# Block products for layer B's input projection from the third head pair on, with their operand sums made in the second pair

## The chip, the cores and the metric

The kernel runs on one core of one Trainium2 chip. The metric is device time in microseconds (us) of one execution, median of several runs. The engines are named as in the profile: PE is the matrix engine (PEld is its loading of the stationary operand), DVE the vector engine, ACT the scalar engine, POOL GpSimd, SP the engine whose queue issues every DMA of this kernel.

## The reference

Two attention layers, each `x + W_out(attn(RMSNorm(x)) * silu(gate))`, on a prompt of 2048 tokens and a sample of 64 tokens, model width 1024:

```python
def project(x, norm_g, w_in, q_g, k_g, n_heads, n_kv):
    h = rms_norm(x, norm_g)
    p = h @ w_in
    q, k, v, gate = jnp.split(p, [wq, wq + wkv, wq + 2 * wkv], axis=-1)
    q = rms_norm(q.reshape(*lead, n_heads, HEAD_DIM), q_g)
    k = rms_norm(k.reshape(*lead, n_kv, HEAD_DIM), k_g)
    ...
def gated_attention_layer(...):
    qp, kp, vp, gp = project(x_p, norm_g, w_in, q_g, k_g, n_heads, n_kv)
    op = prompt_band_attention(qp, kp, vp, past_chunks, bias_fn, sinks)
    y_p = x_p + (op * jax.nn.silu(gp)) @ w_out
    # the same for the sample, against its caches
```

Layer A has 16 query heads on 2 key heads and a window of three chunks of 64 tokens; layer B has 16 heads with keys and values of their own and a window of nine chunks. The new keys and values are outputs too. The change is in layer B's `h @ w_in`, the product of 2112 tokens by 1024 by 4096.

## The kernel before, in words

**Numbers in two parts.** Every large product is made in 32-bit floats split into a high part (rounded to the engine's fast format, `F32R`) and a low part (the rest). `x @ w` is then three products, high by high, high by low and low by high, summed in PSUM. ACT makes the high part, POOL (activations) or DVE (weights) the low part.

**Work of layer B.** The tokens lie in *units*: eight of 256 tokens (two tiles of 128) and one of 64 (the sample, `NU`). `order` is units 0 to 6, the sample, unit 7. The heads go in eight *pairs* (`hp` 0 to 7). One *item* is a unit of a pair, 72 in all. For an item the projection (`project_b`, L513 to L536) makes 512 columns for each tile: 128 of q, k, v and gate each. A tile takes 8 steps of 128 input features with three matmuls each (L527, L528, L529), 48 matmuls of 512 columns for a unit. The activations are the stationary operand, the weights the moving one. The finished tile is evacuated from PSUM by two ACT reads (`evacuate`, L635), then normed and gated.

**Operands.** `load_b` (L542 to L596) loads them. In the first pair each unit's four blocks (two tiles by two halves of the features, named A11, A12, A21, A22) are loaded from layer A's result `x1` into `xraw` (L579), split (L553, L554) into an `xx` buffer and stored split in the DRAM tensor `xo` (L555). Later pairs load the four blocks from `xo` (L549), 512 KB each. There are seven `xx` buffers (`XN`), five of `xraw` (`XR`), three of `wraw` (`WB`), fifteen each of `wh` and `wl` (`WN`).

**Weights.** `load_weights` (L282 to L341) brings a pair's weights in eight chunks of 128 x 512; ACT scales each by the norm's gain and rounds it (L315), DVE makes the low part (L318). Eight of the fifteen buffers hold a pair, so seven chunks of the next pair can be made before the present pair has let go of anything. The first five are given out three jobs early (`EARLY`, `WP`), the rest in the job before.

**Order.** PE's order is written out by the program: attention of an item is taken in steps (`scores` L1244, `values` L1304, `outputs` L1324, driven by `pipeline`), and between two steps a `Filler` emits projection steps up to a mark, so that an item's projection ends two items before its attention. `PACE_B` is the filler work per head and tile. The other engines and the SP queue are ordered by a scheduler. Small jobs for ACT, DVE and POOL wait in a background queue (`bg`) and are given out between the steps of attention. SP's queue is taken in order: what stands behind a DMA that waits, waits too.

**Attention of an item.** For each tile and head: scores into a PSUM buffer of the two named `sb` (L1274, L1275), DVE adds the bias and finds the extremum (L1281), ACT exponentiates (L1285), PE transposes (L743), and a copy brings the result from PSUM (L1321: ACT for the first tile of the unit, DVE for the second). Then the values are multiplied (L1347) and the result goes by way of DVE (L1353) to DRAM.

Of the kernel before, what the change touches and what calls it, by code (L numbers as in the profile page):

```python
# [9 lines left out]
F32 = mybir.dt.float32  # L10
# [5 lines left out]
P = 128  # L16
# [19 lines left out]
XN = 7  # L36
EARLY = 3
# [16 lines left out]
def hybrid_encoder_kernel(  # L54
# [174 lines left out]
    xo = dr.tile([P, 4 * NU + 1, 8 * P], F32, tag="xo", name="xo")  # L229
# [306 lines left out]
    SLOT = {n: i for i, n in enumerate(("A11", "A12", "A21", "A22"))}  # L536
# [5 lines left out]
    def load_b(unit, hp):  # L542
# [13 lines left out]

        if T == TS:
            if hp:
                x.joint = cached("J", 4 * NU)[:, : 8 * P].rearrange("p (k s) -> p k s", k=8)
                return x  # L560
# [3 lines left out]
            def fn():  # L564
                xx = t("xx", [P, 4 * OT], XN, F32R)
                x.joint = v = xx[:, : 8 * P].rearrange("p (k s) -> p k s", k=8)
                split(xx, v[:, :, :TS], v[:, :, TS:], raw, 4 * NU)
# [4 lines left out]
        names = ("A11", "A12", "A21", "A22")  # L572
        raw = {}

        def raws():
            for e in range(2):
                for i in range(2):
                    r = t("xraw", [P, 2 * OT], XR)[:, :512].rearrange("p (k s) -> p k s", k=4)
                    held["last"] = load(r, x1[:, 4 * i : 4 * i + 4, u * UT + e * P : u * UT + e * P + P]).ins  # L579
                    raw["A%d%d" % (e + 1, i + 1)] = r  # L580

        def part(n, src):
            def fn():
                xx = t("xx", [P, 4 * OT], XN, F32R)
                xh, xl = operand(xx)
                split(xx, xh, xl, raw[src], 4 * u + SLOT[n])
                x.op[n] = xh, xl
            return fn

        if hp == 0:  # L590
            raws()
            x.items = [bg.put(0.52, part(n, n)) for n in names]
        else:
            for n in names:
                x.op[n] = operand(cached(n, 4 * u + SLOT[n]))
# [538 lines left out]
    def layer_b():  # L1134
# [4 lines left out]
        def add_unit(hp, unit):  # L1139
# [13 lines left out]
            def weights(*m):  # L1153
                if hp not in st.emit:
                    (st.w[hp],), _, st.emit[hp] = load_weights(1, (w_in_b[hp], 512))
# [41 lines left out]
            filler.total += 8 * (6 if T == UT else 2) * 512 / 2400  # L1197
            it.mark = filler.total
            filler.add(prefetch, weights if u == 0 else None, gen)
# [104 lines left out]
        def values(it, i, h):  # L1304
# [15 lines left out]
            copy = (nc.scalar.copy, nc.vector.tensor_copy)[i]  # L1320
# [36 lines left out]
        def pipeline():  # L1357
# [10 lines left out]
            for x, it in enumerate(its):  # L1368
# [3 lines left out]
                if x + 2 < len(its):  # L1372
                    near = its[x + 2].mark
# [215 lines left out]
```

## Time and profile before

| | |
|---|---|
| median of 3 runs | 2264.24 us (2262.56 to 2265.06) |
| the profiled execution's own time | 2262.1 us |
| its span in the profile | 2260.3 us |
| granted PE clock, mean | 0.997 |
| PE, DVE, ACT, POOL busy | 99%, 63%, 58%, 34% of the span |
| layer B's projection (L527 to L529) | from about 858 us on |
| output projection at the end | about 2110 to 2260 us |

The profile is one execution; times in its views count from the start of the span. Matmuls are pipelined and their ends are modelled, so what a matmul costs is read from the distance between the starts of two that follow each other, not from its duration.

### The profile page before, as it was taken

The numbers are of one execution on the slowest core, as the hardware profiler recorded it, in microseconds if no ns is written. First come the engines' busy times: TensorE is split into PE (matmuls) and PEld (weight loads), VectorE is DVE, ScalarE is ACT, GpSimd is POOL, SyncE is SP. The second block draws the span as 40 slices with busy tenths as digits, with TensorE's granted clock in tenths as the row PEclk, the third lists the DMA queues.
The fourth block names the chain that finished last, engine by engine and source line by source line (L and its number), as shares of the span: only waits on it lengthen the run. The fifth ranks groups of instructions, "written<-read, shape, count | busy, mean of one in ns | idle before, by whom it ended". The sixth has DMA issues, their size and how long they took to land. (4 is left out here: it accounts for less than half of the span.)

```text
span 2260.3 us, 41004 instructions
## 1 busy us (share of the span) xinstructions
PE 2231.6 (99%) x13981; PEld 1908.7 (84%) x13981; DVE 1423.0 (63%) x4168; ACT 1312.7 (58%) x3341; POOL 778.4 (34%) x1153
## 2 busy tenths in 40 slices
PE   8999999999999999999999999999999999999999
PEld 7887888888889998878888888888888888888999
DVE  7779988888785545675655655656556556565211
ACT  7888877777774335664555655545556555454321
POOL 5654533333254445431222222222222212223442
PEclk9999999999999999999999999999999999999999
DMA  8846446754446767554554544544545445443664
GB/s 281 298 144 214 165 139 184 224 179 146 158 121 193 215 188 268 186 182 142 150 148 138 158 139 142 151 145 142 148 140 160 138 137 154 139 125 113 201 182 135
DMA packets 236800, 379.26 MB, mean 168 GB/s; under 512 B 24288, under 2 KB 167024, under 8 KB 236560
## 3 DMA queue, kind: packets, MB, share of 16 engines
q1 hardware_dynamic: 236592, 376.65, 54.4%
q8 instruction: 110, 1.80, 0.3%
q14 instruction: 98, 0.80, 0.1%
HBM read 296.13 MB, written 82.08 MB: 167 GB/s over the span
## 5 line engine op out<-in xcount | busy, mean ns | idle before, releaser
L527 PE MATMUL pj<-wh,xx 128*128 128x512 f32 x1024 | 426.8, 417 | 0.0
L529 PE MATMUL pj<-wh,xx 128*128 128x512 f32 x1024 | 403.6, 394 | 0.0
L528 PE MATMUL pj<-wl,xx 128*128 128x512 f32 x1024 | 403.3, 394 | 0.0
L1285 ACT ACTIVATE p<-p,nm 128x640 f32<-128x640 f32 (+5 forms) x272 | 204.4, 751 | 236.9 <-DVE nm L1281 234.1
L1281 DVE CUSTOM_DVE_ANT_0 p<-sb,BT 128x640 f32<-128x640 f32 (+5 forms) x272 | 196.5, 722 | 173.3 <-PE sb L1275 169.5
L1441 PE MATMUL pj<-xx,wh 128*128 128x264 f32 x1024 | 295.0, 288 | 4.9 <-DVE res L1446 4.8
L389 POOL TENSOR_TENSOR xx<-xraw,xx 128x528 fp32r<-128x528 f32 (+1 forms) x168 | 225.1, 1362 | 202.9 <-ACT xx L388 197.4
L1442 PE MATMUL pj<-xx,wh 128*128 128x264 f32 x1024 | 292.1, 285 | 0.0
L1443 PE MATMUL pj<-xx,wl 128*128 128x264 f32 x1024 | 290.8, 284 | 0.0
L654 POOL TENSOR_TENSOR f<-f,mhalf 128x4 f32<-128x4 f32 (+1 forms) x136 | 137.4, 1011 | 428.9 <-DVE f L653 420.6
L613 PE MATMUL pj<-wh,xx 128*128 128x512 f32 (+1 forms) x624 | 245.9, 394 | 1.3 <-ACT pb L635 1.0
L614 PE MATMUL pj<-wl,xx 128*128 128x512 f32 (+1 forms) x624 | 233.0, 373 | 1.8 <-DVE wl L318 1.8
L615 PE MATMUL pj<-wh,xx 128*128 128x512 f32 (+1 forms) x624 | 234.1, 375 | 0.0
L527 PEld LDWEIGHTS pj<-wh,xx 128*128 128x128 f32 x1024 | 193.0, 188 | 44.9 <-issue 20.1
L529 PEld LDWEIGHTS pj<-wh,xx 128*128 128x128 f32 x1024 | 192.7, 188 | 44.8
L528 PEld LDWEIGHTS pj<-wl,xx 128*128 128x128 f32 x1024 | 193.7, 189 | 23.2
L1441 PEld LDWEIGHTS pj<-xx,wh 128*128 128x128 f32 x1024 | 193.6, 189 | 7.8 <-DVE res L1446 6.0
L635 ACT ACTIVATE pa<-pj,rms 128x384 f32<-128x384 f32 (+1 forms) x219 | 118.1, 539 | 136.7 <-PE pj L529 125.8
L1442 PEld LDWEIGHTS pj<-xx,wh 128*128 128x128 f32 x1024 | 193.3, 189 | 0.2
L1443 PEld LDWEIGHTS pj<-xx,wl 128*128 128x128 f32 x1024 | 193.5, 189 | 0.0
L388 ACT CAST xx<-xraw 128x528 fp32r<-128x528 f32 (+1 forms) x168 | 103.0, 628 | 133.0 <-PE pj L1443 112.9
L1040 ACT ACTIVATE p<-p,nm 128x257 f32<-128x257 f32 (+2 forms) x272 | 134.5, 497 | 73.5 <-DVE nm L1034 61.3
(228 smaller groups left out, 5222.1 us busy)
## 6 DMA issues: line engine op xcount, KB each, us to landing
xx<-xo SPq DMA_DIRECT2D x231, 512.0 KB, 3.6
xx<-xsa SPq DMA_DIRECT2D x88, 512.0 KB, 4.6
xraw<-oga SPq DMA_DIRECT2D x64, 264.0 KB, 3.5
xo<-xx SPq DMA_DIRECT2D x33, 512.0 KB, 4.4
xraw<-ogb SPq DMA_DIRECT2D x64, 264.0 KB, 3.4
xsa<-xx SPq DMA_DIRECT2D x32, 512.0 KB, 4.2
wraw<-in_w_in_b_dram SPq DMA_DIRECT2D x64, 256.0 KB, 3.1
xraw<-in_x_dram SPq DMA_DIRECT2D x40, 256.0 KB, 4.6
```

What stands on the lines that cost most here:

```text
L389: nc.gpsimd.tensor_tensor(xl, rv, xh.bitcast(F32), op=ALU.subtract)
L527: nc.tensor.matmul(ps, xh, wh, start=k == 0, stop=False)
L528: nc.tensor.matmul(ps, xh, wl, start=False, stop=False)
L529: nc.tensor.matmul(ps, xl, wh, start=False, stop=k == KC - 1)
L613: nc.tensor.matmul(ps[:n, :C], xh, wh, start=k == 0, stop=False)
L614: nc.tensor.matmul(ps[:n, :C], xh, wl, start=False, stop=False)
L615: nc.tensor.matmul(ps[:n, :C], xl, wh, start=False, stop=k == KC - 1)
L1281: mi = nc.vector.tensor_tensor_reduce(out=p[:n, :nk], in0=S[:n, o : o + nk], in1=bias[:n, b0 : b0 + nk], op0=ALU.add, op1=ALU.min, scale=1 ...
L1285: ex = nc.scalar.activation(p[:n, :nk], p[:n, :nk], AF.Exp, scale=-1.0, bias=nmh, accum_out=it.sm[:n, 2 * i + h : 2 * i + h + 1],)
L1441: nc.tensor.matmul(ps[:, :OT], wh, oh, start=k == 0, stop=False)
L1442: nc.tensor.matmul(ps[:, :OT], wh, ol, start=False, stop=False)
L1443: nc.tensor.matmul(ps[:, :OT], wl, oh, start=False, stop=k == KC - 1)
```

## The change

The first two pairs (`PLAIN = 2`) are projected as before. From the third pair on, a unit of 256 tokens by 1024 features by 512 columns is treated as a 2 x 2 by 2 x 2 block product and made of seven block products instead of eight (the Strassen-Winograd form). A block product is 4 steps of 3 matmuls with 256 columns, 84 matmuls of 256 columns for a unit. The operands are four sums of the activation blocks (S1 to S4) beside A11, A12 and A22, and four sums of the weight blocks (T1 to T4) beside 11, 21 and 22.

- **Activation sums.** In the second pair each unit's four raw blocks are loaded again from `x1`, DVE makes the four sums in place (L676 of the new file), they are split and stored to slots 4 to 7 of `xo`. A unit's loads are put into the background queue when the next unit is prefetched, and its sums one unit later (`mixed`). From the third pair on a unit loads seven operands of 512 KB instead of four, through the same seven `xx` buffers.
- **Weights.** `block_weights` loads eight raw blocks (three in `wraw`, five in `xraw`), ACT scales block 12 (L588), DVE mixes them in place (L579, 16 half blocks), and seven pieces of two halves are split (ACT L565 or L570, DVE L566 or L571). A pair holds 14 of the 15 buffers.
- **Evacuation.** Two PSUM buffers `pj` take turns, and products of the two tiles share partial sums: P1 is read twice by ACT (once with each tile's scale), P6 and P7 once, P2 once as the result for tile 0's q and k; POOL adds P1 to P6 and to P7; DVE reads P5, P4 and P3 with an addition. P2 goes on top of P1 in its buffer, P7 on top of P6, P4 on top of that, P3 on top of P5.
- **The sample** is made block by block with the same weights, 32 matmuls of 256 columns instead of 16 of 512.
- From the third pair on ACT makes all four copies of L1321, and the pace is 0.875 of `PACE_B`.

```diff
+    def product(ps, xc, parts, p, start):
+        xh, xl = xc.op[OPERAND[p]]
+        for k in range(4):
+            wh, wl = parts(PIECE[p], k)
+            nc.tensor.matmul(ps[:, :256], xh[:, k], wh, start=start and k == 0, ...)
+            nc.tensor.matmul(ps[:, :256], xh[:, k], wl, start=False, ...)
+            nc.tensor.matmul(ps[:, :256], xl[:, k], wh, start=False, ...)
...
+        def sums(u):
+            for dst, a, b, op in (
+                ("A22", "A21", "A22", ALU.add), ("A21", "A11", "A21", ALU.subtract),
+                ("A11", "A22", "A11", ALU.subtract), ("A12", "A12", "A11", ALU.subtract),
+            ):
...
+                    nc.vector.tensor_tensor(raw[dst], raw[a], raw[b], op=op)
...
+            for n, src in (("S1", "A22"), ("S3", "A21"), ("S2", "A11"), ("S4", "A12")):
+                bg.put(0.52, part(n, src, False, u))
+
+        def mixed():
+            held.pop("sums", lambda: None)()
+            v = order.index(unit)
+            if hp == 1 and v < NU:
+                bg.put(0.3, lambda: raws(v))
+                held["sums"] = lambda: sums(v)
...
-            for n in names:
-                x.op[n] = operand(cached(n, 4 * u + SLOT[n]))
+            for n in names if hp < PLAIN else OPERAND.values():
+                x.op[n] = operand(cached(n, 8 * u + SLOT[n]))
+            mixed()
...
+            def gen_blocks():
...
+                A, B = psum("pj", 512, 2), psum("pj", 512, 2)
+                yield from product(A, xc, parts, "P1", True)
+                p1, s1 = scaled(A, r0), scaled(A, r1)
+                yield cost
+                yield from product(B, xc, parts, "P6", True)
+                p6 = scaled(B, r0)
+                nc.gpsimd.tensor_tensor(p6, p1, p6, op=ALU.add)
+                yield cost
+                yield from product(A, xc, parts, "P2", False)
...
-            copy = (nc.scalar.copy, nc.vector.tensor_copy)[i]
+            copy = nc.scalar.copy if i == 0 or it.hp >= PLAIN else nc.vector.tensor_copy
...
+                    if its[x + 2].hp >= PLAIN and len(heads) == 4:
+                        end = c0 + 0.875 * PACE_B * len(heads)
```

**PE, a unit of the fifth pair.** Before, the first matmul of each operand: two PSUM tiles, each filled by 24 matmuls, waits on DMA alone.

```order
L527 MATMUL pj_3756_18210<-wh_3635_17692,xx_3700_17968 128x512 [waits DMAHW3_49]
...
L527 MATMUL pj_3756_18210<-wh_3652_17748,xx_3701_17970 128x512 [waits DMAHW7_49]
...
L743 MATMUL sb_3770_18298<-ident_66,p_3758_18222 128x128 x5
L527 MATMUL pj_3774_18315<-wh_3635_17692,xx_3702_17972 128x512 [waits DMAHW1_49]
L528 MATMUL pj_3774_18315<-wl_3636_17693,xx_3702_17972 128x512
```

Now, the first matmul of each of the seven products P1, P6, P2, P7, P5, P4, P3 of the same unit (`pj_4060`, `pj_4061` and `pj_4080` are PSUM tiles in two buffers):

```order
L626 MATMUL pj_4060_19792<-wh_3864_18843,xx_3999_19491 128x256 [waits DMAHW7_49]
...
L626 MATMUL pj_4061_19793<-wh_3938_19206,xx_4000_19493 128x256 [waits DMAHW3_49,DVE_49]
...
L626 MATMUL pj_4060_19792<-wh_3946_19238,xx_4001_19495 128x256 [waits DMAHW7_49,Activation_49]
...
L626 MATMUL pj_4061_19793<-wh_3953_19274,xx_4002_19497 128x256 [waits DMAHW0_49,Activation_49]
...
L626 MATMUL pj_4080_19901<-wh_3969_19368,xx_4003_19499 128x256 [waits DMAHW1_49,Activation_49]
...
L626 MATMUL pj_4061_19793<-wh_3978_19401,xx_4004_19501 128x256 [waits DMAHW2_49,Activation_49]
...
L626 MATMUL pj_4080_19901<-wh_3985_19429,xx_4005_19503 128x256 [waits DMAHW3_49,DVE_49]
```

Six of the seven products now wait for an evacuation by ACT or DVE as well as for an operand; P2 stands one product, 12 matmuls, behind the end of P1, whose two reads it waits for.

**DVE, where one pair goes over into the next.** Before, between two attention steps (L1281) of that stretch stand the low parts of two or three weight chunks (L318).

```order
L318 SCALAR_TENSOR_TENSOR wl_4358_21073<-wraw_4345_21023,gain_77,wh_4357_21072 128x512 [waits Activation_49]
L318 SCALAR_TENSOR_TENSOR wl_4361_21079<-wraw_4346_21025,gain_77,wh_4360_21078 128x512 [waits Activation_49]
L1321 COPY pl_4366_21096<-sb_4381_21151 128x5x128 [waits PE_49]
L318 SCALAR_TENSOR_TENSOR wl_4364_21085<-wraw_4353_21052,gain_77,wh_4363_21084 128x512 [waits DMAHW6_49,Activation_49]
L1281 ISA p_4383_21166,nm_4373_21121<-sb_4382_21161,BT_88 128x640 [waits PE_49]
```

Now, from one item's output (L1577) to the next attention step (L1505) in the last unit of a pair (`raw` blocks in `wraw` and `xraw`):

```order
L1577 TENSOR_TENSOR o1_4848_23676<-o_4845_23658,gt_4847_23662 128x256 [waits DMAHW6_49,PE_49]
L571 SCALAR_TENSOR_TENSOR wl_4835_23613<-xraw_4743_23183,gain_77,wh_4834_23612 128x256 [waits Activation_49] x2
L579 SCALAR_TENSOR_TENSOR xraw_4743_23183<-xraw_4743_23183,gain_77,wraw_4737_23171 128x256 [waits DVE_49]
L571 SCALAR_TENSOR_TENSOR wl_4837_23619<-xraw_4744_23185,gain_77,wh_4836_23618 128x256 [waits DMAHW2_49,Activation_49]
L579 SCALAR_TENSOR_TENSOR xraw_4743_23183<-xraw_4743_23183,gain_77,wraw_4737_23171 128x256 [waits DVE_49]
L571 SCALAR_TENSOR_TENSOR wl_4837_23619<-xraw_4744_23185,gain_77,wh_4836_23618 128x256 [waits Activation_49]
L579 SCALAR_TENSOR_TENSOR wraw_4737_23171<-xraw_4741_23179,gain_77,wraw_4737_23171 128x256 [waits DVE_49]
L1505 ISA p_4852_23703,nm_4808_23512<-sb_4851_23698,BT_88 128x640 [waits PE_49]
```

Between that output and the next one (the sixth item of a pair's attention) stand 8 rows of L571, 8 of L579 and 6 of L566 on DVE, 8 of L570 and 7 of L565 on ACT.

**SP, where the second pair goes over into the third.** The four operand sums of unit 7 are loaded raw (L658), stored (L649), and the third pair's first operands are loaded (L643) in this order:

```order
L658 DMA xraw_2993_14597<-x1_91 128x4x128 [waits DMAHW1_49,DVE_49]
...
L643 DMA xx_3050_14861<-xo_93 128x1024 [waits DMAHW4_49,DMAHW2_49]
L649 DMA xo_93<-xx_3039_14814 128x1024 [waits DMAHW3_49,Pool_49]
...
L649 DMA xo_93<-xx_3040_14818 128x1024 [waits DMAHW5_49,Pool_49]
...
L643 DMA xx_3051_14863<-xo_93 128x1024 [waits DMAHW1_49]
```

The operand of the fifth product (`xx_3051`) stands behind the store of unit 7's last sum, and the DVE rows of those sums (L676) stand in DVE's order ahead of the attention step that follows.

More of the change, by code (lines that the diff above doesn't have):

```diff
@@ L36 @@
 XN = 7
+PLAIN = 2
 EARLY = 3
@@ L555, in split, with raws, part, fn @@
             store(xo[:, i], xx[:, : 8 * P].bitcast(F32))
+        names = ("A11", "A12", "A21", "A22")
+        raw = {}
+        def raws(u=u):
+            for e in range(2):
+                for i in range(2):
+                    r = t("xraw", [P, 2 * OT], XR)[:, :512].rearrange("p (k s) -> p k s", k=4)
+                    held["last"] = load(r, x1[:, 4 * i : 4 * i + 4, u * UT + e * P : u * UT + e * P + P]).ins
+                    raw["A%d%d" % (e + 1, i + 1)] = r
+        def part(n, src, keep, u=u):
+            def fn():
+                xx = t("xx", [P, 4 * OT], XN, F32R)
+                xh, xl = operand(xx)
+                split(xx, xh, xl, raw[src], 8 * u + SLOT[n])
+                if keep:
+                    x.op[n] = xh, xl
+            return fn
+        def sums(u):
[3 more added lines that the diff above has]
+            ):
+                def fn(dst=dst, a=a, b=b, op=op):
+                    nc.vector.tensor_tensor(raw[dst], raw[a], raw[b], op=op)
+                bg.put(0.6, fn)
+            for n, src in (("S1", "A22"), ("S3", "A21"), ("S2", "A11"), ("S4", "A12")):
[6 more added lines that the diff above has]
+                held["sums"] = lambda: sums(v)
         if T == TS:
             if hp:
[L559 removed]
+                x.joint = cached("J", 8 * NU)[:, : 8 * P].rearrange("p (k s) -> p k s", k=8)
+                mixed()
                 return x
@@ L566, in fn @@
                 x.joint = v = xx[:, : 8 * P].rearrange("p (k s) -> p k s", k=8)
-                split(xx, v[:, :, :TS], v[:, :, TS:], raw, 4 * NU)
+                split(xx, v[:, :, :TS], v[:, :, TS:], raw, 8 * NU)
             x.items.append(bg.put(0.52, fn))
             return x
[L572 to L588, printed above, removed]
         if hp == 0:
             raws()
-            x.items = [bg.put(0.52, part(n, n)) for n in names]
+            x.items = [bg.put(0.52, part(n, n, True)) for n in names]
         else:
-            for n in names:
-                x.op[n] = operand(cached(n, 4 * u + SLOT[n]))
+            for n in names if hp < PLAIN else OPERAND.values():
+                x.op[n] = operand(cached(n, 8 * u + SLOT[n]))
+            mixed()
         return x
```

181 lines of the change are left out of this document (176 added, 5 removed).

## The prediction

> **What bounds the kernel now.** I read the stages first, then PE's waits, then the distance between matmuls, then the costs of the work that moves. The table by stage has, after the length of a stage, the busy time and count of PE, PEld, DVE, ACT and POOL, the granted clock, the DMA share and GB/s. The second and third rows are pairs in the middle of layer B, the last is the output projection at the end.
>
> ```profile
> 900.00:1050.00 150.00, 148.86 (x893) 120.84 (x893) 96.34 (x230) 88.47 (x219) 55.13 (x78) 1.00 0.56 173
> ...
> 1456.00:1600.00 144.00, 143.91 (x863) 117.93 (x861) 86.12 (x229) 79.59 (x203) 32.68 (x62) 1.00 0.48 146
> 1600.00:1744.00 144.00, 143.90 (x870) 117.49 (x870) 84.50 (x226) 79.08 (x202) 31.11 (x59) 1.00 0.48 144
> ...
> 2110.00:2256.00 146.00, 146.00 (x1204) 146.00 (x1203) 22.33 (x51) 29.08 (x46) 59.37 (x46) 1.00 0.59 173
> ```
>
> PE is busy for all of a pair's 144 us at clock 1.00, DVE for 60%, ACT for 55%, DMA for 48%. PE's waits from 1300 to 1900 us confirm it: the longest list entry that is another engine's is 0.3 us in 600.
>
> ```profile
> PEld pj L527 <- issue: 10.6, 32, 0.4
> ...
> PEld sb L1274 <- DVE nm L1281: 0.3, 2, 0.2
> ```
>
> So in layer B a microsecond of PE work taken away is a microsecond of time, as long as no other engine takes over.
>
> **PE, what is removed and added.** The starts of PE's rows give the distance between matmuls. The first two rows below bound six matmuls of 512 columns, the next two are matmuls of 256 columns, all in a pair; the last two bound fifty of 264 columns at the end of the kernel.
>
> ```profile
> 1303.43 0.28 PE L1274 MATMUL sb<-KB,q 128*128 128x256 f32 x1
> 1303.55 0.28 PE L1275 MATMUL sb<-KB,q 128*128 128x256 f32 x1
> 1303.66 0.40 PE L527 MATMUL pj<-wh,xx 128*128 128x512 f32 x1
> ...
> 1305.05 0.71 PE L743 MATMUL sb<-ident,p 128*128 128x128 f32 x5
> 1305.52 0.48 PE L527 MATMUL pj<-wh,xx 128*128 128x512 f32 x1
> ```
>
> ```profile
> 2149.82 0.28 PE L1441 MATMUL pj<-xx,wh 128*128 128x264 f32 x1
> ...
> 2155.91 0.28 PE L1443 MATMUL pj<-xx,wl 128*128 128x264 f32 x1
> ```
>
> 512 columns: (1305.05 - 1303.66) / 6 = 0.2317 us. 264 columns, each with its own weight load: (2155.91 - 2149.82) / 50 = 0.1218 us. The new block products have the shape nearest to the latter: 0.1218 x 256 / 264 = 0.1181 us. A unit's projection goes from 48 x 0.2317 = 11.12 us to 84 x 0.1181 = 9.92 us. 1.20 us less, for 8 units in 6 pairs: 48 x 1.20 = **58 us**. Bounds: at 0.1218 flat a unit takes 10.23 us and the gain is 43 us; at the distance of the 256-column rows, (1303.66 - 1303.43) / 2 = 0.115 us, it takes 9.66 us and the gain is 70 us. The sample keeps its columns (16 x 512 or 32 x 256): nothing. The pace of 0.875 follows the columns (84 x 256 against 48 x 512), so no work slides to the end.
>
> **The evacuations of a unit.** Before, a PSUM tile is read while the other takes 24 matmuls, 24 x 0.2317 = 5.6 us. Now a read has one product, 12 x 0.1181 = 1.42 us, and whatever attention stands between. How fast ACT answers is seen in two tiles of the pair at 1380 us.
>
> ```profile
> 1380.85 0.40 PE L529 MATMUL pj<-wh,xx 128*128 128x512 f32 x1
> ...
> 1389.12 0.40 PE L529 MATMUL pj<-wh,xx 128*128 128x512 f32 x1
> ```
>
> ```profile
> 1381.34 0.58 ACT L635 ACTIVATE pa<-pj,rms 128x384 f32<-128x384 f32 x1 [2.57 <-PE pj L529]
> ...
> 1389.32 0.69 ACT L1321 COPY pl<-sb 128x640 f32<-128x640 f32 x1
> 1389.91 0.59 ACT L635 ACTIVATE pa<-pj,rms 128x384 f32<-128x384 f32 x1
> ...
> 1400.14 0.58 ACT L635 ACTIVATE pa<-pj,rms 128x384 f32<-128x384 f32 x1 [3.20 <-PE pj L529]
> ```
>
> The last matmul ends at 1381.25 and ACT starts at 1381.34; with a copy ahead of it, 1389.52 and 1389.91. So 0.1 to 0.4 us. The costs of the work that moves, and of its nearest relatives, are these groups (busy us, mean ns):
>
> ```profile
> L635 ACT ACTIVATE pa<-pj,rms 128x384 f32<-128x384 f32 x136 | 78.9, 580 | 133.7 <-PE pj L529 125.8 <-PE pj L523 5.9
> L635 ACT ACTIVATE pb<-pj,rms 128x128 f32<-128x128 f32 x136 | 49.1, 361 | 0.0
> L635 ACT ACTIVATE pa<-pj,rms 128x256 f32<-128x256 f32 x83 | 39.2, 472 | 3.0 <-PE pj L615 1.4
> L1321 ACT COPY pl<-sb 128x640 f32<-128x640 f32 x48 | 33.1, 689 | 26.3 <-PE sb L743 25.3
> L553 ACT CAST xx<-xraw 128x512 fp32r<-128x512 f32 x33 | 18.9, 615 | 5.1 <-issue 2.5 <-PE pj L529 2.0
> L315 ACT ACTIVATE wh<-wraw,gain 128x512 fp32r<-128x512 f32 x92 | 64.5, 716 | 19.9 <-DMA wraw<-in_w_in_b_dram 15.3 <-DMA wraw<-in_w_qg_a_dram 2.4 <-PE pj L1442 2.0
> L318 DVE SCALAR_TENSOR_TENSOR wl<-wraw,gain,wh 128x512 fp32r<-128x512 f32 x92 | 70.2, 772 | 12.9 <-ACT wh L315 12.1
> L1321 DVE COPY ph<-sb 128x640 f32<-128x640 f32 x48 | 39.6, 825 | 2.5 <-PE sb L743 1.1
> L652 DVE TENSOR_REDUCE f<-sq 128x4 f32<-128x256 f32 x128 | 53.5, 418 | 51.6 <-ACT sq L651 49.3
> L554 POOL TENSOR_TENSOR xx<-xraw,xx 128x512 fp32r<-128x512 f32 x33 | 43.2, 1331 | 17.7 <-ACT xx L553 17.7
> ```
>
> P1 is read twice: 0.1 to 0.4 + 2 x 0.472 = 1.0 to 1.3 us, under the 1.42 us of P6 behind it, with little to spare. The other six take one read of 256 columns (ACT 0.472, DVE about 0.418): 0.5 to 0.9 us. An exponential ahead (ACT's next largest) would push P1's over the line now and then. I take 0.1 us for a unit, 48 x 0.1 = **5 us**; bounds 0 and 0.1 us at each of seven waits, 34 us. POOL's two additions and the two copies that go from DVE to ACT stand on no chain of PE's own.
>
> **The seam between two pairs.** Here the cover is thinnest. Of 15 weight buffers a pair now holds 14, so nearly all of the next pair's pieces are made in the last unit of the present one. How much is that? A full unit took 1400.14 - 1381.34 = 18.8 us and will take 17.6. Of a pair's 86.1 us of DVE, 8 x 0.772 = 6.2 are weights; the rest over 8 units and a sample that I count as 0.4 is 9.5 us a unit. Two copies go (2 x 0.825) and three reads come (3 x 0.418): 9.1. Into the sixth item of a pair's attention fall 16 half pieces and mixes (half of 0.772 each) and 6 whole ones: 10.8 us. DVE has 19.9 us of work for 17.6 us of PE. ACT: (79.6 - 8 x 0.716) / 8.4 = 8.8; less 2 x (0.580 + 0.361), plus 5 x 0.472 and 2 x 0.689: 10.7; and 7 x 0.615 + 8 x 0.358 = 7.2 on top, 17.9 us. Both are just over PE, and both queues are in order, so scores and evacuations stand behind weight pieces there. I take the 2 us by which DVE is over, at five seams: **10 us**. Bounds: nothing (neighbouring units have 8 us of DVE to spare) and 7 us a seam where ACT and DVE take turns instead of overlapping, 35 us.
>
> **The second pair and its seam.** A unit there moves 4 loads and 4 stores of 512 KB, 4 raw loads of 256 KB and one store of 128 KB, 5.4 MB where it was 2.2, and the SP queue carries it in order.
>
> ```profile
> xx<-xo SPq DMA_DIRECT2D x231, 512.0 KB, 3.6
> ...
> xo<-xx SPq DMA_DIRECT2D x33, 512.0 KB, 4.4
> ...
> xraw<-x SPq DMA_DIRECT2D x33, 256.0 KB, 4.6
> ```
>
> ```profile
> 60.00:70.00 10.00, 9.86 (x65) 8.63 (x65) 8.81 (x30) 8.54 (x25) 8.34 (x16) 1.00 1.00 343
> ```
>
> 5.4 MB in 18.8 us is 287 GB/s, 84% of the 343 GB/s that the trace shows at a DMA share of 1.00. Operands are asked for most of a unit ahead and land in 3.6 us (4.4 or 4.6 for the others), so this is hidden by about 10 us of lead: **3 us**, bounds 0 and 12. From the third pair on it is 3.8 MB in 17.6 us, 216 GB/s: nothing. At the end of the second pair unit 7's raw blocks are loaded only when weight blocks leave `xraw`: 4.6 us to land, DVE's four sums 4 x 0.772, a cast 0.615 and P1's two reads make 9.3 us ahead of P2, while PE has about 5 us to do (P1, P6 and two steps of attention); POOL's four splits at 1.331 us stand ahead of the fifth operand's load. **6 us**, once; bounds 0 and 15.
>
> **The sum.** 2262.1 us of the profiled execution, less 58, plus 10 + 6 + 5 + 3 = 24: 2228 us. The median of three runs lies 2.1 us above that execution, so 2230 us. A measurement of this kernel can tell about 0.2% (4.5 us) from no change.
>
> **The rivals.**
>
> *Nearly all of it shows.* The seams hide in the slack of the neighbours, the reads are always in time. For it: PE waits for nothing now, ACT answers in 0.1 us when free. Against: 19.9 us of DVE in 17.6. Time: 2264 less 52 to 70, 2194 to 2212 us.
>
> *The seams and DMA eat it.* All three bounds at half or more: 20 + 8 + 8 and 10 for the reads against 58 leave about 12 us: 2248 to 2262. For it: ACT and DVE are both over PE at once. Against: only five seams.
>
> *The reads take PE's place as the bound; slower.* Place: the wait of P2 for P1's two reads, and the six like it. It decides at 58 / (48 x 7) = 0.17 us a wait. If every wait is 0.3 us late, 48 x 7 x 0.3 = 101 us, with the seams inside it: 2264 - 58 + 101 = 2307. For it: ACT is busy 10.7 of 17.6 us, its queue is in order, and the cover falls from 5.6 to 1.42 us. Against: two of three kinds of read end at 0.5 to 0.9 us even behind a copy, and most products have attention between them.
>
> *The distance doesn't halve with the columns; slower.* If a matmul costs a fixed part beside its columns, 1.75 times as many instructions cost more than an eighth fewer columns save. Five transposes of 128 columns take 1305.52 - 1305.05 = 0.47 us, 0.094 each; a line from there to 0.2317 at 512 gives 0.140 us at 256 columns, a unit of 84 x 0.140 = 11.8 us, 0.6 us more than now: 48 x 0.6 = 30 us, with 9 for the second pair 2303 us. The row of 264 columns at 0.1218 us speaks against it. The Trainium skill states such a rule, in "TensorE: Matmul & The Clock Gate", Back-to-back issue gap: the spacing in a stream of weight loads and matmuls is set by both, measured as about 81 ns at 128 columns and 131 ns at 512; by a line between these, an estimate, 256 columns take 98 ns and a unit goes from 48 x 131 to 84 x 98 ns, 1.9 us more. The trace here does not agree: 264 columns take 0.526 of the distance of 512, for 0.516 of the columns.
>
> That the change isn't made as described is not a rival: PE's order has the seven products in each of the 48 units.
>
> **How the numbers follow.** My forecast 0.61 (its own range 2212 to 2248), nearly all shows 0.20, eaten 0.09, slower by the reads 0.07, slower by the distance 0.03. Faster by over 0.2%: 0.61 + 0.20 + 0.06 of the eaten = 0.87; within it 0.03; slower 0.10. The range leaves out the lowest of the second case (0.08), the last of the third (0.03) and both slower ones (0.10): 2202 to 2257.
>
> **What would show it.** Right: block matmuls 0.118 us apart; full units about 17.6 us from one P5 to the next inside a pair; PE's waits on DVE and ACT in clusters 130 us apart, at the seams, led by weight pieces. Wrong: a distance of 0.13 us or more; waits of PE for reads in every unit; a second pair longer than 165 us; no waits at the seams.

## The result, and the profile after

| | before | after |
|---|---|---|
| median | 2264.27 us (2262.56 to 2265.06) | 2302.93 us (2301.66 to 2304.55) |
| span of the profiled execution | 2260.3 us | 2302.8 us |
| granted PE clock, mean | 0.997 | 0.987 |
| PE, DVE, ACT, POOL busy | 99%, 63%, 58%, 34% | 96%, 67%, 63%, 39% |

The ratio is 1.0172, 95% interval 1.0155 to 1.0190: 38.7 us slower, where 34 us faster was forecast. PE waits now, and the list of its waits over the whole span says for what (us in total, times, longest). In the kernel before, the same list has no entry at all between 1300 and 1900 us.

```profile
PE pj L626 <- DVE pb L1399: 19.4, 6, 3.7
PE pj L626 <- DMA xx<-xo: 19.1, 2, 18.1
PE pj L626 <- ACT ev L1376: 10.4, 10, 2.1
...
PE pj L626 <- DVE pb L1358: 4.5, 5, 1.0
...
PE pj L1328 <- DVE pb L1411: 4.3, 6, 0.8
```

L1399 is DVE's read of P5, for which P3 waits; L1376 ACT's reads of P1, P6 and P7; L1358 and L1411 are reads at the sample. The second entry is one operand's load. The times repeat pair by pair: the longest waits for L1399 stand at 1323, 1476, 1631, 1784 and 1937 us, one in the projection of each pair's last unit. I call that place a seam. The table by stage (same columns as in the prediction) shows such an end and the stretch behind it.

```profile
1600.00:1620.00 20.00, 18.30 (x153) 16.90 (x152) 17.72 (x44) 15.47 (x37) 7.11 (x10) 1.00 0.53 156
1620.00:1640.00 20.00, 16.33 (x123) 15.43 (x124) 18.18 (x44) 14.45 (x34) 5.62 (x7) 0.91 0.75 226
...
1660.00:1680.00 20.00, 20.00 (x175) 19.56 (x172) 11.57 (x32) 12.73 (x33) 5.68 (x11) 1.00 0.79 244
```

Inside a pair PE has no gap, DVE 11.6 us in 20. At the end of a pair DVE has 18 of 20 and PE loses 1.7 and 3.7 us. What stood in DVE's queue just before the long wait ended:

```profile
1627.42 0.68 DVE L566 TENSOR_TENSOR wl<-xraw,wh 128x512 fp32r<-128x512 f32 x1
1628.02 0.48 DVE L579 SCALAR_TENSOR_TENSOR wraw<-xraw,gain,wraw 128x256 f32<-128x256 f32 x1
...
1628.86 0.82 DVE L1505 CUSTOM_DVE_ANT_0 p<-sb,BT 128x640 f32<-128x640 f32 x1
...
1629.61 0.48 DVE L579 SCALAR_TENSOR_TENSOR wraw<-xraw,gain,wraw 128x256 f32<-128x256 f32 x1
1630.00 0.48 DVE L1399 SCALAR_TENSOR_TENSOR pb<-pj,rms,ev 128x256 f32<-128x256 f32 x1
```

and PE's rows at the same time, the last of P5, the last of P4 and the first of P3:

```profile
1624.44 0.28 PE L628 MATMUL pj<-wh,xx 128*128 128x256 f32 x1
...
1626.59 0.28 PE L628 MATMUL pj<-wh,xx 128*128 128x256 f32 x1
1630.54 0.58 PE L626 MATMUL pj<-wh,xx 128*128 128x256 f32 x1 [3.67 <-DVE pb L1399]
1630.92 0.42 PE L627 MATMUL pj<-wl,xx 128*128 128x256 f32 x1
1631.13 0.42 PE L628 MATMUL pj<-wh,xx 128*128 128x256 f32 x1
```

P5's read, half a microsecond long, starts 5.3 us after P5's last matmul has ended (1624.72) and 3.1 us after P4's, the one product that covers it. DVE is busy for all of PE's wait (3.64 of 3.67 us): weight pieces (L566) and mixes (L579) of the next pair, and attention's own rows between them, are queued ahead of the read. Then the matmuls stand 0.21 us apart, not 0.12: the granted clock has halved (0.51 from 1630.4 to 1633.8 us, 1.00 behind it).

To see where the time went, I took the last output of each pair (the addition that ends `outputs`) from one pair to the next. The rows for the third pair, after:

```profile
1227.37 0.43 DVE L1577 TENSOR_TENSOR o<-o,gt 128x256 f32<-128x256 f32 x1 [1.12 <-PE o L1571]
...
1377.55 0.42 DVE L1577 TENSOR_TENSOR o<-o,gt 128x256 f32<-128x256 f32 x1
```

So it took 150.2 us. For all pairs, in us (the first from its first output; the rows from once on are kernels of the next section):

| pair | 1 | 2 | 3 | 4 | 5 | 6 | 7 | 8 |
|---|---|---|---|---|---|---|---|---|
| before | 139.9 | 152.9 | 151.0 | 150.1 | 150.5 | 150.5 | 150.5 | 155.7 |
| after | 147.4 | 175.8 | 150.2 | 153.0 | 154.8 | 153.1 | 152.9 | 151.9 |
| once | 145.3 | 172.3 | 143.1 | 143.3 | 143.4 | 143.6 | 143.1 | 151.4 |
| late7 | 145.5 | 155.6 | 151.4 | 154.5 | 152.9 | 154.3 | 152.9 | 150.9 |
| no_sums | 140.7 | 154.2 | 150.9 | 154.4 | 152.9 | 154.3 | 152.8 | 150.7 |
| flat | 143.8 | 157.4 | 150.8 | 150.0 | 150.1 | 150.3 | 149.9 | 151.8 |
| flat_small | 144.3 | 159.4 | 157.2 | 159.7 | 160.0 | 160.3 | 160.3 | 151.5 |
| mix_first | 143.8 | 156.3 | 148.3 | 147.7 | 149.0 | 149.8 | 147.6 | 151.3 |
| no_mix | 143.9 | 156.2 | 145.5 | 145.8 | 145.8 | 147.4 | 145.8 | 150.9 |
| t2_early | 143.7 | 155.3 | 148.1 | 147.4 | 147.5 | 149.4 | 148.0 | 151.7 |

The first two pairs lost 7.5 and 22.9 us, the next five 11.4 together; the last gained 3.8, but the stretch from the last output to the end of the span lost 4.2 (155.5 us before, 159.7 after). The first output itself stands between 901.4 and 910.3 us in these executions (904.1 after, 909.6 in once), though none of the edits is ahead of it; so one execution's total can hold up to 9 us that are not the edit's, and I go by the pairs where the two differ.

### The profile page after: what moved, and what is told of

Same layout as the page of the kernel before. It is cut to its first block, busy times and chain, and to the rows that moved or that the text cites. A ratio compares the mean times of both kernels' runs of the same rounds, so it can differ in the third digit from the quotient of the medians.

```text
span 2302.8 us, 46023 instructions
## 1 busy us (share of the span) xinstructions
PE 2206.1 (96%) x15805; PEld 1992.7 (87%) x15805; DVE 1547.2 (67%) x4428; ACT 1440.4 (63%) x3619; POOL 908.8 (39%) x1281
## 5 line engine op out<-in xcount | busy, mean ns | idle before, releaser
L626 PE MATMUL pj<-wh,xx 128*128 128x256 f32 x1344 | 405.5, 302 | 57.0 <-DVE pb L1399 19.4
L628 PE MATMUL pj<-wh,xx 128*128 128x256 f32 x1344 | 382.6, 285 | 0.0
L627 PE MATMUL pj<-wl,xx 128*128 128x256 f32 x1344 | 382.0, 284 | 0.0
L626 PEld LDWEIGHTS pj<-wh,xx 128*128 128x128 f32 x1344 | 257.9, 192 | 80.6 <-DVE pb L1399 20.7
L1505 DVE CUSTOM_DVE_ANT_0 p<-sb,BT 128x640 f32<-128x640 f32 (+5 forms) x272 | 196.5, 723 | 112.2 <-PE sb L1499 109.3
L627 PEld LDWEIGHTS pj<-wl,xx 128*128 128x128 f32 x1344 | 258.7, 192 | 0.0
L628 PEld LDWEIGHTS pj<-wh,xx 128*128 128x128 f32 x1344 | 257.8, 192 | 0.0
L769 POOL TENSOR_TENSOR f<-f,mhalf 128x4 f32<-128x4 f32 (+1 forms) x136 | 143.8, 1058 | 158.6 <-DVE f L768 153.8
L1672 DVE TENSOR_TENSOR res<-pj,res 128x264 f32<-128x264 f32 x128 | 55.0, 430 | 192.0 <-PE pj L1669 188.8
```

Source lines behind the costliest of these rows:

```text
L626: nc.tensor.matmul(ps[:, :256], xh[:, k], wh, start=start and k == 0, stop=False, skip_group_check=not start)
L627: nc.tensor.matmul(ps[:, :256], xh[:, k], wl, start=False, stop=False, skip_group_check=not start)
L628: nc.tensor.matmul(ps[:, :256], xl[:, k], wh, start=False, stop=k == 3, skip_group_check=not start)
L1505: mi = nc.vector.tensor_tensor_reduce(out=p[:n, :nk], in0=S[:n, o : o + nk], in1=bias[:n, b0 : b0 + nk], op0=ALU.add, op1=ALU.min, scale=1 ...
```

## The experiments

Theory: the block products are as fast as forecast; the next pair's weight pieces delay PSUM reads at the five seams, and unit 7's sums delay the third pair's first operand. Rivals: late reads in every unit; the clock falling by itself; the first block weights being late. Times are medians; ratios are to the kernel before.

**once**: one set of block weights; the fourth to eighth pair's own weights are left out.

```diff
+                    elif hp > PLAIN:
+                        st.w[hp], st.emit[hp] = st.w[PLAIN], lambda *m: None
```

> The changed kernel, but the fourth to eighth pair use the third pair's weight pieces: their raw blocks aren't loaded, mixed or split (so those pairs' projections are made with the wrong weights; the work on PE is the same). Theory, weight pieces ahead of the PSUM reads in DVE's and ACT's queues at the seams: at the first of the five seams the waits are 3.7 + 0.9 + 0.6 us, at the other four 2.1 + 3.7 + 0.9 + 0.8, and behind each wait of over 2 us the matmuls stand 0.21 us apart instead of 0.118 for 3.2 us, 1.4 us more. That is 6.6 + 4 x 10.3 = 48 us: 2303 - 48 = 2255. Rival, reads too late in every unit, whatever stands in the queues: the waits stay where a product has little attention behind it; 2303 to 2290. Rival, the clock falls because the block products are denser, without any wait: the granted clock stays at 0.987, 2290 or more.

Measured 2254.51 us, ratio 0.9956 (0.9939 to 0.9973): the theory's 2255. A pair now takes 143.1 us, as these rows show for the third, and in the stretch that had the seam PE is nearly full at clock 1.00:

```profile
1227.26 0.42 DVE L1579 TENSOR_TENSOR o<-o,gt 128x256 f32<-128x256 f32 x1 [1.13 <-PE o L1573]
...
1370.39 0.42 DVE L1579 TENSOR_TENSOR o<-o,gt 128x256 f32<-128x256 f32 x1
```

```profile
1600.00:1620.00 20.00, 20.00 (x171) 19.02 (x170) 12.42 (x34) 12.25 (x31) 6.82 (x13) 1.00 0.74 232
1620.00:1640.00 20.00, 19.78 (x176) 18.43 (x177) 11.82 (x35) 11.51 (x31) 7.70 (x15) 1.00 0.70 234
```

Both rivals fall: the same products wait for almost nothing when no weights are made (0.9 us a pair), and the clock stays up at the seams. The five seams cost 7.1 + 9.7 + 11.4 + 9.5 + 9.8 = 47.5 us (row after less row once, third to seventh pair). One detail of the expectation was wrong. Of four waits of 2.1 us in the kernel after only the one at 1590 us has slow matmuls behind it; all five of 3.7 us have. Three stretches of 1.4 us were counted too many, so the waits and stretches add up to 44 us, not 48, and that 2255 was met to the microsecond is partly luck.

**late7**: unit 7's sums in the third pair.

```diff
-            if hp == 1 and v < NU:
+            if hp == 1 and v < NU - 1:
...
+            if hp == 2 and v == 1:
+                bg.put(0.3, lambda: raws(NU - 1))
+                held["sums"] = lambda: sums(NU - 1)
```

> The changed kernel, but the last unit's raw blocks, sums and split operands are made in the second unit of the third pair instead of the second pair's last unit. Theory: the 18.1 us wait for the third pair's first operand is the chain raw loads that need the xraw buffers that hold weight blocks, four sums, four splits, stores ahead of that operand's load in SP's queue. With it go 18.1 us and a slow stretch of 1.4 us, and what comes next is small, since the weight pieces for the first product are there 30 us early: 2303 - 19 = 2284. Rival: the operand is late anyway, since seven operands of 512 KB cannot be prefetched through seven buffers at a change of pair; the wait stays at 8 us or more, 2293 or more. Rival: weight pieces on DVE and ACT (19.8 of 20 us there) take the wait over: 2293 or more, with waits on DVE instead of the DMA.

Measured 2286.42 us, ratio 1.0104 (1.0089 to 1.0119): 16.5 us gained of 19. The DMA wait is gone and the second pair takes 155.6 us instead of 175.8. The chain in the kernel after, first the stage by the table, then SP's rows, then DVE, POOL and PE:

```profile
1140.00:1160.00 20.00, 13.66 (x79) 10.80 (x75) 19.76 (x47) 14.16 (x33) 7.79 (x8) 0.98 0.27 74
1160.00:1180.00 20.00, 6.42 (x46) 6.06 (x48) 7.35 (x12) 5.83 (x12) 7.73 (x7) 0.59 0.73 244
```

```profile
1158.78 0.98 SPq L658 DMA_DIRECT2D xraw<-x  x2
...
1168.10 0.33 SPq L649 DMA_DIRECT2D xo<-xx  x1
1168.52 1.21 SPq L643 DMA_DIRECT2D xx<-xo  x2
```

```profile
1164.40 0.69 DVE L676 TENSOR_TENSOR xraw<-xraw,xraw 128x512 f32<-128x512 f32 x1 [2.81 <-DMA xraw<-x]
```

```profile
1166.81 2.67 POOL L648 TENSOR_TENSOR xx<-xraw,xx 128x512 fp32r<-128x512 f32 x2
```

```profile
1173.58 0.58 PE L626 MATMUL pj<-wh,xx 128*128 128x256 f32 x1 [18.06 <-DMA xx<-xo]
```

DVE is full until about 1160 us (19.76 of 20, 13.0 of it weight pieces and mixes), and the raw blocks could be loaded only as those left `xraw`: the last loads go out at 1159 and DVE has them at 1164.4. The first sum, ACT's cast and POOL's first split took until 1168.1, when its store went out. Behind this store, which SP waited for, stood the load of the next pair's first operand (the row at 1168.52), which PE had 5 us later.

**no_sums**: the activation sums are left out; the plain blocks' slots are loaded again in place of S1 to S4.

```diff
-            if hp == 1 and v < NU:
+            if hp < 0:
...
-                x.op[n] = operand(cached(n, 8 * u + SLOT[n]))
+                x.op[n] = operand(cached(n, 8 * u + SLOT[n] % 4))
```

> The changed kernel without its activation sums: nothing is loaded, added, split or stored for them in the second pair, and from the third pair on the products take the plain blocks in place of S1 to S4 (so the results of those pairs are wrong; loads, matmuls and reads are as many as in the changed kernel). Theory: the sums' whole price is what the outputs lose up to the third pair's first unit, 7.9 us at its start, 2.0 in it and 21 at its seam: 2303 - 31 = 2272. Rival, the loss at the second pair's end is from the first block weights, not from the sums: 2290 or more.

Measured 2274.95 us, ratio 1.0061 (1.0041 to 1.0082). The sums cost 28 us by the medians and 28.3 by the first two rows of the table (6.7 and 21.6). Beside late7 those two rows are 4.8 and 1.4 us shorter: the price of the other seven units' sums.

**late7_once**: both.

> Both edits in one: the last unit's sums in the third pair, and the fourth to eighth pair on the third pair's weight pieces (their own are left out, so those pairs' projections are made with the wrong weights). Theory, the seams' weight pieces and the last unit's sums are two losses with nothing in common: both gains add up, 2303 - 48 - 16.5 = 2238; a pair between seams takes 143.3 us from its last output to the next pair's, as in the run with one set of weights, and the second pair 155.6 as in the run with the late sums. Rival, they share something (the first seam's weight pieces were late behind the sums, or the reverse): 2245 or more.

Measured 2235.55 us, ratio 0.9878 (0.9861 to 0.9894). The two losses add up, as expected (2238). Without them the block products are worth 27 us beside the kernel before; the other units' sums are still paid in that, five of six sets of weights are not.

**pool_low**: the low parts of T1 to T4 on POOL.

```diff
-                    nc.vector.tensor_tensor(wl, rv, wh.bitcast(F32), op=ALU.subtract)
+                    nc.gpsimd.tensor_tensor(wl, rv, wh.bitcast(F32), op=ALU.subtract)
```

> The changed kernel, but POOL instead of DVE makes the low part of the four mixed weight pieces (T1 to T4, two halves each). Theory, DVE has 19.5 of 20 us of work at a seam: 8 x 0.68 = 5.4 us leave DVE there, the waits on DVE (3.7, 0.9, 0.8) fall under 1 us together and with the longest goes one stretch of slow matmuls (1.4); ACT's 2.1 us and its slow stretch stay. 5 x 5.5 = 27 us less: 2276. Rival, POOL is the next that is late (1.33 us for a piece, 8 of them in two units in which it has 6 to 7 of 20 us of work): PE waits for pieces from POOL, 2295 to 2310. Rival, the scarce thing at the seam is ACT's high parts, not DVE: same time, 2300.

Measured 2321.71 us, ratio 1.0258 (1.0242 to 1.0273): worse by 19 us, and not as the rival put it, since PE waits for no piece from POOL. DVE itself became slower. The groups of after and then of this run (busy us, mean ns), and two rows of this run at one time:

```profile
L571 DVE SCALAR_TENSOR_TENSOR wl<-xraw,gain,wh 128x256 fp32r<-128x256 f32 x48 | 22.1, 483 | 0.0
L566 DVE TENSOR_TENSOR wl<-wraw,wh 128x512 fp32r<-128x512 f32 x30 | 20.9, 701 | 2.3 <-ACT wh L565 2.2
...
L566 DVE TENSOR_TENSOR wl<-xraw,wh 128x512 fp32r<-128x512 f32 x18 | 12.8, 732 | 0.0
L579 DVE SCALAR_TENSOR_TENSOR wraw<-wraw,gain,xraw 128x256 f32<-128x256 f32 x12 | 5.6, 473 | 0.0
```

```profile
L571 DVE SCALAR_TENSOR_TENSOR wl<-xraw,gain,wh 128x256 fp32r<-128x256 f32 x48 | 39.3, 842 | 2.5 <-ACT wh L570 2.5
...
L579 DVE SCALAR_TENSOR_TENSOR wraw<-wraw,gain,xraw 128x256 f32<-128x256 f32 x12 | 15.1, 1261 | 0.0
```

```profile
1468.46 2.46 DVE L579 SCALAR_TENSOR_TENSOR wraw<-wraw,gain,xraw 128x256 f32<-128x256 f32 x1
```

```profile
1469.38 1.26 POOL L566 TENSOR_TENSOR wl<-wraw,wh 128x512 fp32r<-128x512 f32 x1
```

L566's 20.9 + 12.8 = 33.7 us left DVE; this group of L571 gave back 17.2 and this one of L579 9.5 (L579's other groups got 1.1 shorter, the cast at L1463 7.3 longer). DVE's busy time over the span is 1553.3 us, where it was 1547.2 with the work still on it. A DVE instruction of 0.47 us that meets POOL's takes 2.46: it starts while POOL's instruction before this one runs (L769, until 1469.4) and ends 0.3 us after this one. The Trainium skill has this in "SBUF — State Buffer", Who interferes with whom: a DVE instruction with two inputs in SBUF contends with a GpSimd instruction that reads SBUF, and the lock on the ports that the two share is exclusive. These rows agree.

**prescale, flat, prescale_flat**, all with the sums as in late7. flat gives out the background jobs in smaller parts; prescale scales all raw blocks first (on ACT) and mixes blocks of 512 columns.

```diff
-                    bg.share(BL, BP_)
+                    bg.share(*((1.2, 8) if it.hp >= PLAIN else (BL, BP_)))
```

```diff
-                for j in range(2):
-                    nc.vector.scalar_tensor_tensor(
-                        raw[dst, a][:, j], raw[src_, a][:, j], g(int(src_[0]), a, j), raw[other, a][:, j], ...
+                nc.vector.tensor_tensor(raw[dst, a], raw[src_, a], raw[other, a], op=op)
...
+        todo += [scale(b, a) for b in ("11", "12", "22") for a in two]
```

> The kernel with the last unit's sums in the third pair, its weights as in the changed kernel, but from the third pair on the background queue is given out in smaller parts: at each of the eight calls of an item the larger of 1.2 us and an eighth of what waits, instead of 1.8 us and a quarter. Same work, same engines. Theory, bunching: a quarter of 17 us of jobs stands ahead of a read at once; in parts of 2 us the waits of 2.1 and 3.7 us fall below 1 and their slow stretches go; five seams by 5 us: 2286 - 25 = 2261. Rival, load: DVE has 37 of 40 us in the last two items however the jobs are cut, and pieces that come later are waited for by the next pair's first products: 2283 to 2300, with waits on wl.

> The kernel with the last unit's sums in the third pair, and its weights made another way, with the same products in the same order: ACT scales all eight raw blocks in place, DVE mixes whole blocks of 512 columns, and every piece is one cast and one subtraction. Scalings, the first mix and one piece (11 jobs) are given out three jobs ahead. A pair's weights take DVE 22 x 0.68 = 15.0 us instead of 16 x 0.48 + 6 x 0.87 + 8 x 0.70 = 18.5, of these 13.6 in the last two items; ACT keeps 14 x 0.61 = 8.5 us there instead of 12. Theory, DVE's and ACT's load in the last two items of a pair is the loss (19.5 of 20 us on DVE): 4.9 us less on DVE take the 3.7 us wait and its slow stretch down to nothing or 1 us; five seams by 4 to 6 us: 2286 - 25 = 2261. Rival, it is the bunching of jobs ahead of a read, not the load: eleven jobs three jobs ahead make ACT's 2.1 us wait longer; 2280 to 2295.

> The last two edits together. If load and bunching both count: 2286 - 35 = 2251, nearer to the 2238 of the run without weights than either alone. If only the load counts, as the run with scaled blocks alone (2261 by that theory); if only the bunching, as the run with smaller parts alone. Slower than both if pieces now come too late for the next pair's first products, with PE waiting on wl at its start.

Measured: flat 2269.55 us, ratio 1.0033 (1.0020 to 1.0046), 17 us less than late7; prescale 2293.37, 1.0130 (1.0115 to 1.0145), 7 more; both 2269.90, 1.0024 (1.0010 to 1.0038). flat got 17 of the 25 us that it was expected to gain; prescale, and both together, came out as their rivals have it. So how many jobs stand ahead of a read at once counts. In flat the wait for P5's read falls from 3.7 to 2.0 us at most:

```profile
PE pj L626 <- DVE pb L1402: 9.2, 5, 2.0
PE pj L626 <- ACT ev L1379: 8.3, 12, 1.3
```

What is left of it is still a batch. Right ahead of the read (L1402), behind which PE went on after 1.77 us, stand four half mixes:

```profile
1455.51 0.88 DVE L579 SCALAR_TENSOR_TENSOR xraw<-xraw,gain,wraw 128x256 f32<-128x256 f32 x2
1456.30 0.88 DVE L579 SCALAR_TENSOR_TENSOR wraw<-xraw,gain,wraw 128x256 f32<-128x256 f32 x2
1457.09 0.48 DVE L1402 SCALAR_TENSOR_TENSOR pb<-pj,rms,ev 128x256 f32<-128x256 f32 x1
```

prescale takes load from DVE but puts scalings in a bunch on ACT, and there ACT's entry is the longest; P5's read is still waited for by up to 3.4 us:

```profile
PE pj L618 <- ACT ev L1371: 21.6, 19, 3.7
PE pj L618 <- DVE pb L1394: 15.4, 5, 3.4
```

A smaller load on DVE that comes as a larger bunch on ACT gains nothing.

**flat_small, pre_flat_small**: still smaller parts (0.7, 12).

> As the run with smaller parts, but still smaller: the larger of 0.7 us and a twelfth of what waits, from the third pair on. Theory, bunching: with parts of one or two jobs the 1.8 to 2.0 us wait of P3 for P5's read falls under 1 us; five seams by 2 to 3 us: 2270 - 12 = 2258, pairs of 147.5 us. Rival, load: what is given out later is lacking later; PE waits for wl or reads in the next pair's first unit, 2268 to 2285.

> The run with scaled blocks and the same still smaller parts (0.7 us or a twelfth). Theory, bunching: there the longest wait is P2's for ACT's reads (2.9 us) behind two scalings; with one scaling at a time it falls to 1 us or less, and DVE has 3.5 us less at each seam than in the run beside it: 2270 - 20 = 2250, pairs of 146.5 us. Rival, load or lateness: 2265 or more.

Measured 2320.56 us, 1.0253 (1.0235 to 1.0271), and 2336.40 us, 1.0311 (1.0286 to 1.0335). The rival was right, and stronger than I put it. Now PE waits for the pieces themselves, in flat_small at their high parts:

```profile
PE pj L626 <- ACT wh L565: 20.7, 15, 2.8
PE pj L626 <- ACT wh L570: 10.2, 5, 2.1
```

**flat_all, mix_first**: smaller parts (1.2, 8) in all pairs; block 12 mixed ahead of the first piece.

```diff
-        todo += [piece("11", a, "11", True) for a in two]
         todo += [f(a) for a in two for f in (scaled_12, lambda a: mix("12", "22", "12", a, ALU.subtract))]
+        todo += [piece("11", a, "11", True) for a in two]
```

> As the run with smaller parts (1.2 us or an eighth), but in all pairs of layer B, not from the third on. Theory: the price of the sums that is left (143.8 and 157.4 us for the first two pairs where the kernel before has 139.9 and 152.9) is bunching of the same kind, and goes by half: 2270 - 4 = 2266. Rival: it is the bytes and POOL's splits in the second pair; same time, 2270.

> As the run with smaller parts, but the jobs that need no free weight buffer (scaling and mixing block 12) come ahead of the first piece, so four half mixes (1.9 us of DVE) and four half scalings (1.8 us of ACT) leave the last two items of a pair and one half piece enters them. Theory, load and bunching at the seam: five seams by 1 to 2 us: 2262. Rival: ACT's scalings three jobs ahead make the wait for ACT's read there longer by as much: 2270.

Measured 2266.22 us, 1.0009 (0.9998 to 1.0021), and 2263.21 us, 0.9989 (0.9975 to 1.0004): 3 and 6 us, the sizes that were expected. But in mix_first the waits for P5's read are hardly shorter than in flat (8.9 us in five, where it was 9.2). What went are five waits of 1.0 us at the sample (4.6 us in all), and three of the five stretches at half clock. Two are left, at 1597 and 1747 us; those pairs take 149.0 and 149.8 us, the others 147.6 to 148.3.

**no_mix**: flat, with DVE's mixes left out.

```diff
-                for j in range(2):
+                for j in range(0):
                     nc.vector.scalar_tensor_tensor(
                         raw[dst, a][:, j], ...
```

> The run with smaller parts from the third pair on (1.2 us or an eighth; 2269.6), with DVE's mixing of the weight blocks left out: all 16 half mixes of a pair are gone (so the pieces are of unmixed blocks and the results of those pairs are wrong), ACT's scalings, casts and all low parts stay. Theory, DVE's load at the seam is what is left there (150.0 us for a pair beside 143.3 without weights): 16 x 0.48 = 7.7 us of DVE go, the waits on DVE with them; 6 seams by 4 to 5 us: 2243. Rival, ACT's queue holds the rest (its waits of 1.3 and 2.4 us, and the stretches of slow matmuls behind them): 2260 or more.

Measured 2245.85 us, 0.9940 (0.9919 to 0.9961): 24 us less than flat. The waits for P5's read have gone, ACT's are as long as in flat:

```profile
PE pj L626 <- ACT ev L1379: 9.0, 13, 1.3
...
PE pj L626 <- DVE pb L1402: 0.4, 1, 0.4
```

Pairs 3 to 7 go from 150.2 us on average to 146.1. So with smaller parts the mixes on DVE decide 4.1 of the 6.9 us a pair that flat has over once (143.3), and that is what it had at each seam: the 1.8 us wait for P5's read, 1.4 us by the half-clock stretch behind it (five in flat, none here) and a wait of 0.9 us at the sample. Since the mixes are also the batch that stood ahead of that read, this run does not tell DVE's load from the batch. The other 2.8 us should be ACT's work and the low parts, which this run leaves in; that was not tried.

**all_mix, t2_early**: flat_all with mix_first; then T2's raw halves also mixed early, into two `res` buffers.

```diff
+        def second(a):
+            def fn():
+                r = t("res", [P, 2 * OT], 2)[:, :512].rearrange("p (k c) -> p k c", k=2)
+                raw["T2", a] = r
...
+        todo += [second(a) for a in two]
```

> The two edits that each came to the time of the kernel before, together: smaller parts in all pairs, and block 12 mixed ahead of the first piece. Theory, the first acts in the two pairs ahead of the blocks (3 us), the second at the seams (6 us), so they add up: 2269.6 - 9 = 2260, 0.2% under the kernel before. Rival: the shares in the second pair's last unit set what its seam costs in both; 2263 to 2266.

> As the last, but T2's raw halves are mixed into two buffers of the kernel that are free then (res), so that the mix needs no weight piece ahead of it and is done three jobs before the next pair: another four half mixes (1.9 us of DVE) leave the last two items of a pair. Theory, load at the seam: six seams by 1 to 2 us less than the last run: 2252, faster than the kernel before by 0.5%. Rival, the jobs three items ahead (seven now) make a seam of their own there: as the last run or slower, 2260 to 2268.

Measured 2262.15 us, 0.9996 (0.9984 to 1.0008), and 2257.90 us, 0.9978 (0.9966 to 0.9989). The two edits did not add up (7 of 9 us), and t2_early got 4 of the 10 us that it was expected to gain. It is the one version with all of the computation that is clearly faster than both kernels: by 5 us (0.2%) than the one before, by 45 than the one after. Its waits for P5's read are still 8.4 us in five, but none of them has a stretch at half clock behind it.

## Why the prediction was wrong

The sum missed by 73 us (forecast -34, measured +39). In the two profiled executions the difference is 42.5 us: 38.0 in the pairs, 4.2 behind the last output, 0.3 ahead of the first. Its terms:

1. **PE's saving and the reads (forecast 58 - 5 = 53 us; measured 40, of which 4 are lost again behind the last output).** The mechanism was right. Inside a product eight steps from matmul to matmul take 1584.28 - 1583.33 = 0.95 us, 0.119 each:

```profile
1583.33 0.28 PE L626 MATMUL pj<-wh,xx 128*128 128x256 f32 x1
...
1584.28 0.28 PE L628 MATMUL pj<-wh,xx 128*128 128x256 f32 x1
```

   I had 0.118. A unit saves 48 x 0.2317 - 84 x 0.119 = 1.13 us, 9.0 a pair. The pairs of once show 7.9, 6.8, 7.1, 6.9 and 7.4, and the last 4.3, 40 us together. The waits for reads that once keeps are 0.9 us a pair:

```profile
PE pj L1330 <- DVE pb L1413: 4.2, 6, 0.8
...
PE pj L626 <- ACT ev L1378: 1.4, 6, 0.3
```

   That is near my 0.8, but by luck: the full units' reads (L1378) are 0.2 us of it, and 0.7 are at the sample (L1413), for which I had put nothing. The remaining 1 us a pair isn't settled. And "no work slides to the end" was wrong: behind the last output once has 1270 matmuls of the output projection, where the kernel before has 1246, 24 x 0.122 = 2.9 us more, and that stretch is 3.8 us longer. So the last pair's 4.3 us are nearly all given back.

2. **The seams (forecast 10 us, bound 35; measured 47.5).** This is the step that failed: "I take the 2 us by which DVE is over, at five seams". First, the work was undercounted. A pair's weights take DVE 16 x 0.48 + 6 x 0.97 + 8 x 0.71 = 19.2 us (19.7 by the busy time of all their groups), nearly all in the last two items; I priced only one item's share, 10.8, and halved a row of 512 columns for 256 (0.386) where 0.48 is measured. I also took stretches of 144 us for pairs, which take 150.5. Second, and more: the loss isn't how far a queue is over. Counted in full, two items of 9.1 us and these 19.2 against 2 x 17.6 us of PE are 2.2 us over, no more than I had; a seam costs 9.5. A product covers a read for one product, 1.42 us, as I had worked out; a quarter of the waiting jobs stands in the queue ahead of it. (POOL's addition, which I had on no chain of PE's, feeds P5's read too; at the seam shown it was done by 1625.0 us, so it did not decide.) flat shows it (17 us with the same work). How much of the rest is load alone is open: no_mix takes it away together with the last batch, and prescale, with less load on DVE and a larger batch on ACT, gained nothing. I had both facts, the cover and the in-order queue, and put them only into a rival with a wait in every unit. And each 3.7 us wait was followed by a stretch at half clock, for which the sum had no term.

3. **The second pair and its seam (forecast 9 us, bounds 0 to 27; measured 30.4).** The chain at the seam is the one described, raw loads behind weight blocks, sums, splits, loads behind stores. I put it at the fifth operand and P2, and let it begin when the seam begins. It delays the first operand, since the first loads of the third pair stand behind the store of the first sum and not only behind the last; and it starts late, since the weight blocks that hold `xraw` wait in a DVE queue that is full for 20 us. late7 shows 16.5 us of it (20.2 by the second pair's row). The other units' sums cost 6 us (late7 beside no_sums, first two pairs), where I had 3.

The rival "reads take PE's place" gives 2307 us, close to the 2303 measured, but by a path that the trace does not show: its waits in every unit aren't there, and once takes them all away. The rival by distance falls with the 0.119 us. "Nearly all shows" and "eaten" kept the seams small as I did.

Of what I said would show me wrong, "a second pair longer than 165 us" came (175.8); the clusters at the seams, which I had put under right, came with five times the price, and 153 us apart, not 130.

## What to carry to other kernels

A saving on the bound engine counts only if the other engines' worst stretch, not their mean, has room for the new work: count all jobs of a rare burst, by the rows of their own shape, in the items where buffers allow them. Where a read of PSUM shares an in-order queue with background jobs, its delay is the batch that can stand ahead of it; compare that with the work that covers the read, and give the jobs out in parts smaller than that cover, but not later than they are needed (beside parts of 1.8 us and a quarter, 1.2 us and an eighth gained 17 us here, 0.7 us and a twelfth lost 34). Before a chain of loads is put at a change of stage, ask what still holds its buffers, and which load of the next stage stands behind its stores.

## What the hardware showed

**The clock after a short wait.** The trace gives each stretch at half clock as 3.41 us at 0.50 (or two and four times that), and its matmuls stand 0.21 us apart instead of 0.12. Not every wait is followed by one: three of the four of 2.14 us in the kernel after were not. In flat the slow stretch starts after the third matmul behind a wait of 1.77 us:

```profile
1457.62 0.39 PE L626 MATMUL pj<-wh,xx 128*128 128x256 f32 x1 [1.77 <-DVE pb L1402]
...
1459.03 0.41 PE L626 MATMUL pj<-wh,xx 128*128 128x256 f32 x1
1459.24 0.41 PE L627 MATMUL pj<-wl,xx 128*128 128x256 f32 x1
```

The starts of these stretches lie on one grid in each run. In the kernel after they are at 1323.2, 1476.8, 1589.5, 1630.4, 1784.0 and 1937.6 us: 45, 78, 90, 135 and 180 times 3.413 us behind the first. The Trainium skill, "TensorE: Matmul & The Clock Gate", What's actually happening, speaks of windows of about 3.4 us that run freely, with half clock after an idle one. The length and the free run agree; that the window has to be idle does not. I laid the grid over PE's idle time from 1190 to 2000 us in fourteen of the runs. Of the windows at full clock with 0.7 us of idle or more, 53 were followed by one at half clock, and these had 1.73 us of idle or more; 163 were not, and had 1.77 or less. So here about half a window of waiting is enough. That is why three of the waits of 2.14 us cost nothing more: the one at 1436.6 us is cut by the grid into 1.4 and 0.75. In t2_early no window at full clock has more than 1.66 us, and none of its seams has a stretch at half clock. Such a wait is dearer than it looks: 3.2 us at 0.213 instead of 0.119 are 1.4 us more, and by these two executions the five stretches that t2_early is spared (5 x 1.4 = 7 us) are more than half of the 12 us between it and flat.

**DVE beside POOL.** Work moved from DVE to POOL came back on DVE: in pool_low 33.7 us left it, and its busy time is 6 us longer all the same (1547.2 to 1553.3 us).
